# Two feed-forward chunks go up by Strassen's seven products, and the four banks of the ways down become one tile

## The chip, the cores and the metric

The kernel runs on one core of a Trainium2 chip. The metric is the time of one execution on the device in microseconds (us), lower is better. A core has TensorE (PE, matmuls), VectorE (DVE), ScalarE (ACT), GpSimd (POOL) and SyncE (SP, which here only issues DMAs). Each has its own instruction queue, worked off in order, and they wait for each other by semaphores.

## The reference

x is 512 tokens of 1024 features in float32. Two layers; in each a half-step SwiGLU feed-forward, a mixer (an mLSTM in layer 0, a chunked gMLP in layer 1), a second feed-forward and a gated per-layer embedding (PLE), each followed by a layer norm:

```python
for i in range(DEPTH):
    x = layer_norm(DN_ALPHA * x + 0.5 * swiglu_ffn(x, ffn1_wgu[i], ffn1_wd[i]), ...)
    x = layer_norm(DN_ALPHA * x + mix, ...)                  # mlstm_mixer or gmlp_mixer
    x = layer_norm(DN_ALPHA * x + 0.5 * swiglu_ffn(x, ffn2_wgu[i], ffn2_wd[i]), ...)
    x = layer_norm(DN_ALPHA * x + sigmoid(x @ ple_wg[i] + ple_bg[i]) * (p[i] @ ple_wp[i]), ...)

def swiglu_ffn(x, w_gu, w_d):
    g, u = jnp.split(x @ w_gu, 2, axis=-1)
    return (jax.nn.silu(g) * u) @ w_d                        # hidden width 2816
```

## The kernel before, in words

**Products.** A float32 product is made of three matmuls (mm3, lines 277 to 281): high by high, low by high and high by low, where the high part (whi, xh, fhi) is the value rounded to fp32r and the low part (wlo, xl, flo) the rest. The high part is an ACT copy (weights L198, others L284), the low part a DVE subtraction (L207, L285), or, where a stage asks for it, an ACT copy of the negative and an accumulating DMA that POOL issues (L205).

**Weights.** The class Weights streams all weights in one list, W.order: SP loads raw tiles (wraw of 1 MB, three buffers; wquarter of 512 KB for the ways down), fill() splits the next entry as soon as its pool (main, rows, extra and others) has a free pair of tiles, take() hands a pair to PE's code and release() gives it back and calls fill(). The order in which the code calls these sets the order on every queue; there is no scheduler behind it.

**A feed-forward** (ffn, L827) has 22 blocks of 128 hidden columns, in chunks of 2, 4, 4, 4, 4 and 4 blocks. Going up, each block is two tiles (gate and up) of 24 matmuls of 512 columns into a PSUM bank of ps_up (fps); ACT applies silu (sg, L856), DVE multiplies (h, L860). Going down, the h of a whole chunk is a 2 by 2 problem in halves of tokens and output features: class Group (L765) makes it by Strassen's seven products, r = 0 to 6. form() adds quarters of h on DVE (L792 to L797) and splits them (fhi, flo), the weights' quarters are added in place by Weights.forms (L109 to L115), product() runs 12 matmuls (6 in chunk 1, whose chunk before has two blocks) into two PSUM banks (gps), and add() adds a finished product to x (xt), bank by bank (residual, L626 or L628). The seven products of chunk c − 1 stand between the up tiles of chunk c: after the up tile i comes add() of the product before, then silu or multiplication, then product(i) and form(). The last chunk goes down plainly (down, L654): for each of four token tiles 24 matmuls into two banks (dps), then two residuals, a norm and transposes of x back to the form that PE needs (turn_x, L490; DVE steps of the norm to come, affine, L620 and L621, run in the next feed-forward's chunk 1).

**PSUM.** Four banks are for going up (up0 to up3), four are tiles dn0 to dn3, handed out by dn_bank (L295) to groups, to down, to turn_x and to the mixers' and embedding's tiles (vps, gvps L1311, gps of the embedding L1527). Even products of a group write one pair of banks and odd ones the other: product r uses the pair of product r − 2 (and, but for r = 0, 1 and 3, goes on adding to what stands there).

**mLSTM** makes its own way down by a Group for each head, between the tiles of the next head's projections, with the convolution (L1003) on DVE.

## Time and profile before

| what | value |
|---|---|
| median of 3 runs | 2227.38 us (2226.92 to 2227.43) |
| span of the profiled execution | 2225.4 us |
| granted TensorE clock | 9 tenths or more in each of 40 slices |
| DMA | 253.57 MB, mean 114 GB/s |
| a feed-forward chunk of four blocks with a group (219 to 282 us): PE, DVE, ACT busy | 63.00, 40.74, 21.98 us |

The span is that of the profiled execution itself; what the runs' time has beyond it, 2.0 us against their median, lies around it. In the profile a row of a timeline has the start and the duration, the engine, the line of the kernel, the operation and the tiles (written <- read) with their shapes; `x2` joins two instructions that follow each other. The bracket names how long the engine stood idle before and what ended that. A matmul's duration (0.39 us) is longer than the distance to the next one, since matmuls overlap; time on PE is read from the starts.

### The profile page before, as it was taken

The numbers are of one execution on the slowest core, as the hardware profiler recorded it, in microseconds if no ns is written. First come the engines' busy times: TensorE is split into PE (matmuls) and PEld (weight loads), VectorE is DVE, ScalarE is ACT, GpSimd is POOL, SyncE is SP. The second block draws the span as 40 slices with busy tenths as digits, with TensorE's granted clock in tenths as the row PEclk, the third lists the DMA queues.
The fourth block names the chain that finished last, engine by engine and source line by source line (L and its number), as shares of the span: only waits on it lengthen the run. The fifth ranks groups of instructions, "written<-read, shape, count | busy, mean of one in ns | idle before, by whom it ended". The sixth has DMA issues, their size and how long they took to land.

```text
span 2225.4 us, 26475 instructions
## 1 busy us (share of the span) xinstructions
PE 2214.4 (100%) x10517; PEld 1856.1 (83%) x10517; DVE 1557.3 (70%) x2280; ACT 922.2 (41%) x1308; POOL 104.3 (5%) x135
## 2 busy tenths in 40 slices
PE   9999999999999999999999999999999999999998
PEld 8888888888888888888888888888888888888887
DVE  5666667776776786666687766666788778666677
ACT  4333336464646443333345333335345453333332
POOL 1000000111101100000000000000001100000000
PEclk9999999999999999999999999999999999999999
DMA  7422223466847444332233422223437743332221
GB/s 230 130 95 88 95 86 100 100 143 140 160 117 154 130 133 128 98 106 63 99 123 111 134 92 90 95 85 97 140 76 152 164 129 130 117 114 86 85 86 57
DMA packets 206308, 253.57 MB, mean 114 GB/s; under 512 B 5812, under 2 KB 160564, under 8 KB 206184
## 3 DMA queue, kind: packets, MB, share of 16 engines
q1 hardware_dynamic: 168080, 211.83, 29.4%
q0 software_dynamic: 31488, 25.35, 8.4%
q10 hardware_dynamic: 6616, 14.69, 2.0%
q8 instruction: 83, 1.36, 0.2%
q14 instruction: 41, 0.34, 0.0%
HBM read 224.58 MB, written 2.11 MB: 102 GB/s over the span
## 4 chain that ended last, share of the span: by engine, by line
PE 98%; ACT 1%; DMA 0%; DVE 0%; issue 0%; SPq 0%; DVEq 0%
PE fps L279 13%; PE fps L280 13%; PE fps L281 13%; PE gps L279 8%; PE gps L281 8%; PE gps L280 8%; PE dps L279 2%; PE dps L281 2%; PE dps L280 2%; PE gups L279 1%; PE vps L279 1%; PE zps L279 1%; PE zps L281 1%; PE vps L281 1%; PE gvps L279 1%; PE gups L280 1%
## 5 line engine op out<-in xcount | busy, mean ns | idle before, releaser
L279 PE MATMUL fps<-xh,whi 128*128 128x512 f32 x1312 | 510.7, 389 | 0.0
L280 PE MATMUL fps<-xl,whi 128*128 128x512 f32 x1312 | 510.4, 389 | 0.0
L281 PE MATMUL fps<-xh,wlo 128*128 128x512 f32 x1312 | 510.4, 389 | 0.0
L207 DVE TENSOR_TENSOR wlo<-wraw,whi 128x1024 fp32r<-128x1024 f32 (+1 forms) x292 | 352.7, 1218 | 147.9 <-ACT whi L198 146.8
L198 ACT ACTIVATE whi<-wraw 128x1024 fp32r<-128x1024 f32 (+1 forms) x340 | 352.2, 1048 | 179.0 <-PE fps L280 81.6
L207 DVE TENSOR_TENSOR wlo<-wquarter,whi 128x1024 fp32r<-128x1024 f32 (+1 forms) x140 | 156.5, 1118 | 218.2 <-ACT whi L198 218.2
L281 PEld LDWEIGHTS fps<-xh,wlo 128*128 128x128 f32 x1312 | 246.2, 188 | 51.3
L279 PEld LDWEIGHTS fps<-xh,whi 128*128 128x128 f32 x1312 | 246.3, 188 | 51.2
L280 PEld LDWEIGHTS fps<-xl,whi 128*128 128x128 f32 x1312 | 246.3, 188 | 50.6
L198 ACT ACTIVATE whi<-wquarter 128x1024 fp32r<-128x1024 f32 (+1 forms) x140 | 136.3, 974 | 279.8 <-PE gps L281 209.0
L281 PE MATMUL gps<-whi,flo 128*128 128x512 f32 x644 | 251.1, 390 | 0.0
L279 PE MATMUL gps<-whi,fhi 128*128 128x512 f32 x644 | 251.1, 390 | 0.0
L280 PE MATMUL gps<-wlo,fhi 128*128 128x512 f32 x644 | 251.0, 390 | 0.0
L628 DVE TENSOR_TENSOR xt<-xt,gps 128x512 f32<-128x512 f32 x302 | 193.2, 681 | 0.7 <-PE gps L281 0.7
L856 ACT ACTIVATE sg<-fps 128x512 f32<-128x512 f32 x80 | 47.9, 598 | 228.5 <-PE fps L281 224.3
L281 PEld LDWEIGHTS gps<-whi,flo 128*128 128x128 f32 x644 | 120.9, 188 | 25.7
L280 PEld LDWEIGHTS gps<-wlo,fhi 128*128 128x128 f32 x644 | 120.9, 188 | 25.5
L279 PEld LDWEIGHTS gps<-whi,fhi 128*128 128x128 f32 x644 | 120.9, 188 | 25.5
L284 ACT ACTIVATE fhi<-h 128x512 fp32r<-128x512 f32 (+1 forms) x140 | 80.5, 581 | 142.8 <-DVE h L793 54.4
L285 DVE TENSOR_TENSOR flo<-h,fhi 128x512 fp32r<-128x512 f32 (+1 forms) x140 | 87.2, 635 | 42.9 <-ACT fhi L284 42.9
L598 POOL TENSOR_TENSOR rs<-rs,eps_pow 128x1 f32<-128x1 f32 x32 | 20.6, 643 | 1573.6 <-DVE rs L597 1573.6
L501 ACT ACTIVATE xf<-xps,cols 128x128 f32<-128x128 f32 x160 | 59.8, 454 | 53.5 <-PE xps L496 53.5
(306 smaller groups left out, 3625.8 us busy)
## 6 DMA issues: line engine op xcount, KB each, us to landing
wraw<-in_ffn_wgu_dram SPq DMA_DIRECT2D x79, 1024.0 KB, 6.3
wquarter<-in_ffn_wd_dram SPq DMA_DIRECT2D x64, 512.0 KB, 3.7
wraw<-in_ml_w_in_dram SPq DMA_DIRECT2D x24, 1024.0 KB, 5.5
wlo<-wraw POOLq DMA_DIRECT2D x48, 512.0 KB, 6.6
wraw<-in_gm_w_in_dram SPq DMA_DIRECT2D x15, 1024.0 KB, 5.6
wraw<-in_ffn_wgu_dram SPq DMA_DIRECT2D x17, 512.0 KB, 4.0
wraw<-in_ffn_wd_dram SPq DMA_DIRECT2D x8, 1024.0 KB, 4.9
wraw<-in_ml_w_out_dram SPq DMA_DIRECT2D x8, 1024.0 KB, 5.0
```

Of the source, the lines that this page charges most:

```text
L198: self.nc.scalar.activation(hi[:, s], src[:, s], AF.Copy)
L207: self.nc.vector.tensor_sub(lo[:, s], src[:, s], hi[:, s].bitcast(F32))
L279: mm(ps, st[0], mv[0], start=start, stop=False, skip_group_check=more)
L280: mm(ps, st[0], mv[1], start=False, stop=False, skip_group_check=more)
L281: mm(ps, st[1], mv[0], start=False, stop=stop, skip_group_check=more)
L284: sca.activation(hi, src, AF.Copy)
L285: vec.tensor_sub(lo, src, hi.bitcast(F32))
L501: sca.activation(xf[:, k], ps[:, k], AF.Identity, scale=col("ln_g", norm.at + 4 * g + k), bias=col("ln_b", norm.at + 4 * g + k))
L598: pool.tensor_tensor(rs[:, 1:2], rs[:, 0:1], eps_pow, op=OP.pow)
L628: vec.tensor_add(dst, dst, ps)
L856: sca.activation(sg, ps, AF.Silu)
```

## The change

1. Going up in chunks 4 and 5 (UP_FROM): two blocks at a time are a pair, x's features and tokens are halved, and gate and up weights of two blocks form the 2 by 2 problem. Each of seven products is 24 matmuls of 256 columns into half a bank at a time (class UpPair), so 168 of them stand for 96 of 512 columns. The weights' combinations are made in place on the raw loads by DVE (up_forms, four of the seven need additions); the combinations of x by UpForms, in steps of DVE and ACT in chunk 3, two after each up tile from the fourth on (FORM_AT), and last() behind that chunk's last tile. take() collects the sums out of the banks; a group's products stand after every second product going up.
2. Five of the seven lows of each pair (UP_BY_DMA) are made by an ACT copy and an accumulating DMA.
3. The four PSUM tiles dn0 to dn3 become one tile, dn_all, of four banks. dn_bank hands out a slice of it, dn_pair two neighbouring banks, and a group's add() takes both banks of a product in one DVE instruction of 128x2x512.
4. The rows' pool has two buffers for three, a further one (rowsx) is opened late in chunk 5, and the norm's tiles (Norm) are made there too.

```diff
+    def up_forms(self, g, u):
...
+        def s2():
+            vec.tensor_add(quarter(u, 0), quarter(u, 0), quarter(u, 1))
+            vec.tensor_sub(quarter(g, 0), quarter(u, 0), quarter(g, 0))
+            return quarter(g, 0), (g,)
...
+        def s3():
+            vec.tensor_sub(quarter(u, 0), quarter(u, 1), quarter(g, 0))
+            return quarter(u, 0), (u,)
...
+        def s4():
+            vec.tensor_sub(quarter(g, 1), quarter(g, 1), quarter(g, 0))
+            return quarter(g, 1), (g,)
...
+        for _, make in made:
+            self.in_place.add(make)
+        self.by_dma.update(made[r][1] for r in UP_BY_DMA)
+        return [("main", js, make) for js, make in made]
...
-                if low == "dma" and make not in self.in_place:
+                if make in self.by_dma or low == "dma" and make not in self.in_place:
                     self.nc.scalar.activation(lo[:, s], src[:, s], AF.Copy, scale=-1.0)
                     self.nc.gpsimd.dma_start(lo[:, s], src[:, s], accum_op=OP.add)
...
-    def dn_bank(name, pin=False):
+    dn_all = ps_dn.tile([P, 4, 512], F32, name="dn_all", tag="dn_all")
+    def dn_bank(name):
         i = next(i for i in dn_order if i not in pinned.values())
         dn_order.remove(i)
         dn_order.append(i)
...
+    def dn_pair(name):
+        i = next(i for i in dn_order if not {i, i ^ 1} & set(pinned.values())) & 2
+        for j in (i, i + 1):
...
+        pinned[id(pair)] = i
+        pinned[id(pair), 1] = i + 1
+        return pair
...
         del W.order[first:]
         for c, n in enumerate(FFN_CHUNKS):
             down_w = deque(forms(c - 1) if c else ())
+            if c >= UP_FROM:
+                products = []
+                for b in range(starts[c], starts[c] + n, 2):
+                    products += W.up_forms(*(W.add_load(kp(wgu)[:, :, c0:c0 + 2 * P], 2) for c0 in (b * P, HID + b * P)))
+                for s, product in enumerate(products):
+                    W.order.append(product)
+                    if s % 2 == 0:
+                        W.order.append(down_w.popleft())
+                continue
             for i in range(2 * n):
...
-                self.banks.append([dn_bank("gps", True) for _ in range(2)])
-            for e, ps in enumerate(self.banks[r % 2]):
+                self.banks.append(dn_pair("gps"))
+            pair = self.banks[r % 2]
+            for e in range(2):
                 for k in range(self.half):
                     i, j = (e, k) if self.by_tokens else (k, e)
-                    mm3(ps, [a[:, i, j * P:(j + 1) * P] for a in f], [a[:, k] for a in w],
+                    mm3(pair[:, e], [a[:, i, j * P:(j + 1) * P] for a in f], [a[:, k] for a in w],
                         k == 0 and r in (0, 1, 3), k == self.half - 1, r not in (0, 1, 3))
...
             i, j = self.TO[r]
-            for e, ps in enumerate(self.banks[r % 2]):
-                residual(2 * i + e, j, ps, r in self.first)
-                if r >= 5:
-                    unpin(ps)
-    def ffn(layer, k, rows, prepare=None):
-        with stage_pool("forms", 2) as fpool, stage_pool("quarters", Q_BUFS) as qpool, stage_pool("hpool", 2) as hpool:
+            pair = self.banks[r % 2]
+            dst = xt[:, 2 * i:2 * i + 2, j * 512:(j + 1) * 512]
+            if r in self.first:
+                vec.scalar_tensor_tensor(dst, dst, ALPHA, pair, op0=OP.mult, op1=OP.add)
...
+            def x22():
+                for i, s in enumerate(halves):
+                    joined(a[i], 1, 1, s)
+            def t3():
+                for i, s in enumerate(halves):
+                    vec.tensor_sub(b[:, s], a[i], b[:, s])
+            def t1():
+                for i, s in enumerate(halves):
+                    vec.tensor_sub(a[i], a[i], c[:, s])
+            def split_t1():
+                for i, s in enumerate(halves):
+                    split(self.t1[0][:, s], self.t1[1][:, s], a[i])
+            self.steps = [
+                x22, lambda: joined(b, 0, 1), t3, lambda: joined(c, 0, 0), lambda: vec.tensor_add(c, b, c),
+                lambda: sca.activation(f32r(self.t2, late, "whi"), c, AF.Copy), t1, split_t1]
+            def last():
+                split(*self.t3, b)
+                d = [tmp_tile("x_d").rearrange("p (k t) -> p k t", k=2) for _ in range(2)]
+                for i, s in enumerate(halves):
+                    joined(d[i], 1, 0, s)
+                    vec.tensor_sub(d[i], d[i], c[:, s])
+                vec.tensor_sub(f32r(self.t2, late, "wlo"), c, self.t2[0].bitcast(F32))
+                hi, lo = f32r(self.t4, pool, "f1"), f32r(self.t4, pool, "f0")
+                for i, s in enumerate(halves):
+                    split(hi[:, s], lo[:, s], d[i])
+            self.last = last
+            self.right = [self.quarter(0, 0), self.quarter(1, 0), self.t2, self.t1, self.t3,
+                          self.quarter(1, 1), self.t4]
...
+        def product(self, r):
+            w = W.take()
+            c = (0, 1, 0, 3, 0, 3, 0)[r]
+            if r == c:
+                self.at[c], bank = up_bank("ups", True)
+                self.bank[c] = bank.rearrange("p (e c) -> p e c", e=2)
+            ps = self.bank[c]
+            for e in range(2):
+                for k in range(4):
+                    mm3(ps[:, e], [a[:, k, e * P:(e + 1) * P] for a in w], [a[:, k] for a in self.right[r]],
+                        r == c and e == 0 and k == 0, k == 3, r != c or e > 0)
...
+        def take(self, r):
+            bank, part = self.bank, self.part
+            if r in (0, 2, 3):
+                part[r] = tmp_tile("us").rearrange("p (e c) -> p e c", e=2)
+                sca.activation(part[r], bank[3 if r == 3 else 0], AF.Copy)
+            elif r in (1, 5):
+                g = part[r // 5 * 2]
+                vec.tensor_add(g, g, bank[1 if r == 1 else 3])
+                sca.activation(g, g, AF.Silu)
+                if r == 5:
+                    self.gated(1, g, part[3])
+            elif r == 4:
+                vec.tensor_add(part[3], part[3], bank[0])
+            else:
+                self.gated(0, part[0], bank[0])
+            if r in (1, 5, 6):
+                up_held.remove(self.at[{1: 1, 5: 3, 6: 0}[r]])
+        def gated(self, t, g, u):
+            s = slice(256 * t, 256 * t + 256)
+            h = g if self.h is None else self.h[:, :, s]
+            vec.scalar_tensor_tensor(h, g, 0.5, u, op0=OP.mult, op1=OP.mult)
+            if self.h is None:
+                split(*(a[:, :, s] for a in self.parts), h)
...
+            def up_products(c, n, h):
+                nonlocal norm
+                pairs = []
+                for s in range(7 * n // 2):
...
+                    pair.product(r)
+                    group.add()
+                    if r == 5 and h is None:
+                        pair.parts = [W.spare(name).rearrange("p (b t) -> p b t", b=2) for _ in range(2)]
+                        hs.extend([a[:, e] for a in pair.parts] for e in range(2))
+                    pair.take(r)
+                    W.release()
+                    if s % 2 == 0:
+                        group.product()
+                        W.release(kind="rows")
+                        group.form()
+                    if c == LAST and b == n - 2:
+                        if r == 2:
+                            W.open("rowsx", late, 1)
+                        elif r == 4:
+                            norm = Norm(layer, k)
             for c, n in enumerate(FFN_CHUNKS):
                 if c < LAST:
                     h = hpool.tile([P, 4, SEQ], F32, name="h", tag="h")[:, :n]
                 elif prepare is not None:
                     prepare()
-                for i in range(2 * n):
+                if c == UP_FROM - 1:
+                    formed = UpForms(tpool, late)
+                if c >= UP_FROM:
+                    up_products(c, n, h if c < LAST else None)
+                for i in range(2 * n if c < UP_FROM else 0):
                     b = i // 2
                     ps = project()
...
                         group.form()
                     if c == 1 and i < 3:
                         run_affine()
+                    if formed is not None and i >= FORM_AT:
+                        formed.step()
+                        formed.step()
+                if c == UP_FROM - 1:
...
+                        formed.step()
+                    formed.last()
                 if c < LAST:
                     group = Group(h, fpool, c == 0)
                     group.form()
                     group.form()
                 if c == 0:
...
-                if c == 1:
-                    norm = Norm(layer, k)
             return down(hs, False, norm, lazy=layer == 0, defer=prepare is not None)
...
     def ffn_stage(layer, k):
-        with stage_pool("rows", 3) as rows:
-            W.open("rows", rows, 3)
-            ffn(layer, k, rows)
+        with stage_pool("rows", 2) as rows, stage_pool("late") as late:
+            W.open("rows", rows, 2)
+            ffn(layer, k, rows, late)
             W.close("rows")
```

Two places in the order of the built programs. The first is PE at product 1 of the group in layer 0's first feed-forward, chunk 2 (fps: up tile; gps: the banks of the group; whi, wlo, fhi, flo: weights and h forms; in brackets the engines whose count it waits for). Before:

```order
L281 MATMUL fps_938<-xh_87,wlo_773 128x512
L279 MATMUL gps_966<-whi_784,fhi_869 128x512 [waits Activation_49]
L280 MATMUL gps_966<-wlo_785,fhi_869 128x512
L281 MATMUL gps_966<-whi_784,flo_870 128x512 [waits DVE_49]
L279 MATMUL gps_966<-whi_784,fhi_869 128x512
```

After:

```order
L320 MATMUL fps_906<-xh_88,wlo_768 128x512
L318 MATMUL dn_all_86<-whi_807,fhi_846 128x512 [waits DVE_49,Activation_49]
L319 MATMUL dn_all_86<-wlo_808,fhi_846 128x512
L320 MATMUL dn_all_86<-whi_807,flo_847 128x512
L318 MATMUL dn_all_86<-whi_807,fhi_846 128x512
```

The product's first matmul has gained a wait for DVE: its count is that of the add of product 0, which reads the two other banks of dn_all. Before, the DVE wait stands at the third matmul alone, for the form's low. All later up matmuls stand behind it on PE.

The second is DVE at the end of chunk 3 of the same feed-forward, from the last product's add to the low of the next group's first h form (flo_1723 before, flo_1719 now). Before:

```order
L628 TENSOR_TENSOR xt_86<-xt_86,gps_1331 128x512
L628 TENSOR_TENSOR xt_86<-xt_86,gps_1332 128x512
L860 SCALAR_TENSOR_TENSOR h_1303<-sg_1666,fps_1690 128x512
L207 TENSOR_TENSOR wlo_1719<-wraw_1567,whi_1718 128x1024
L285 TENSOR_TENSOR flo_1723<-h_1303,fhi_1722 128x512
L285 TENSOR_TENSOR flo_1727<-h_1303,fhi_1726 128x512
```

After:

```order
L896 TENSOR_TENSOR xt_87<-xt_87,dn_all_86 128x2x512
L1072 SCALAR_TENSOR_TENSOR h_1266<-sg_1640,fps_1671 128x512
L246 TENSOR_TENSOR wlo_1699<-wraw_1490,whi_1698 128x1024
L324 TENSOR_TENSOR xl_89<-x_wlo_1269,xh_88 128x4x256
L915 TENSOR_TENSOR x_d_1704<-xh_88,xl_89 128x512
L946 TENSOR_TENSOR x_d_1704<-x_d_1704,x_f0_1270 128x512
L915 TENSOR_TENSOR x_d_1705<-xh_88,xl_89 128x512
L946 TENSOR_TENSOR x_d_1705<-x_d_1705,x_f0_1270 128x512
L947 TENSOR_TENSOR t_wlo_1710<-x_f0_1270,t_whi_1612 128x1024
L324 TENSOR_TENSOR t_f0_1713<-x_d_1704,t_f1_1712 128x512
L324 TENSOR_TENSOR t_f0_1713<-x_d_1705,t_f1_1712 128x512
L324 TENSOR_TENSOR flo_1719<-h_1266,fhi_1718 128x512
```

Two adds have become one of 128x2x512, and eight instructions of last() (xl, x_d, t_wlo, t_f0) have come between the last up weights' low and the form's low that PE waits for.

More of the change, by code (lines that the diff above doesn't have):

```diff
@@ L45 @@
 PLE_EXTRA = 3
+UP_BY_DMA = (1, 2, 4, 5, 6)
 class Weights:
@@ L363, in ffn_weights @@
         first = len(W.order)
-        for at in range(HB):
-            if at in (0, HB - 1):
+        for at in range(starts[UP_FROM]):
+            if at == 0 or at == starts[UP_FROM] - 1:
                 W.add(*((kp(wgu)[:, :, c0:c0 + P], [slice(None)]) for c0 in (at * P, HID + at * P)))
@@ new lines, in add, with __init__, joined, f32r @@
+            if r >= 5:
+                unpin_pair(pair)
+    class UpForms:
+        def __init__(self, pool, late):
+            f32 = lambda at, tag: at.tile([P, 4, 256], F32, name="x_" + tag, tag=tag)
+            a = [tmp.tile([P, 2, 256], F32, name="x_a", tag="pad", bufs=3) for _ in range(2)]
+            b, c = f32(late, "wlo"), f32(pool, "f0")
+            both = act.tile([P, 2, 4, 256], F32R, name="t1", tag="gb")
+            self.t1, self.t2, self.t4 = [both[:, 0], both[:, 1]], [], []
+            self.t3 = self.quarter(0, 1)
+            whole, halves = slice(0, 4), (slice(0, 2), slice(2, 4))
+            def joined(dst, k, t, s=whole):
+                vec.tensor_add(dst, *(p[:, s].bitcast(F32) for p in self.quarter(k, t)))
+            def f32r(to, at, tag):
+                to.append(at.tile([P, 4, 256], F32R, name="t_" + tag, tag=tag))
+                return to[-1]
+            def x22():
[26 more added lines that the diff above has]
+                          self.quarter(1, 1), self.t4]
+        def quarter(self, k, t):
+            return [a[:, 4 * k:4 * k + 4, 256 * t:256 * t + 256] for a in (xh, xl)]
+        def step(self):
+            if self.steps:
+                self.steps.pop(0)()
@@ L829, in ffn @@
+    def ffn(layer, k, rows, late, prepare=None):
+        with stage_pool("forms", 2) as fpool, stage_pool("quarters", Q_BUFS) as qpool, \
+                stage_pool("hpool", 2) as hpool, stage_pool("tforms") as tpool:
             name = (layer, k)
@@ L1460, in ffn_ple @@
     def ffn_ple(i, last):
-        with stage_pool("rows", 3) as rows:
-            W.open("rows", rows, 3)
+        with stage_pool("rows", 2) as rows, stage_pool("late") as late:
+            W.open("rows", rows, 2)
             ph, pl = [], []
@@ L1550, in ffn_ple @@
                 norm.apply(TB - 1)
-                for kind in ("rows", "rows2", "extra"):
+                for kind in ("rows", "rowsx", "rows2", "extra"):
                     W.close(kind)
```

69 lines of the change are left out of this document (51 added, 18 removed).

## The prediction

> **What bounds the kernel now.** I read the busy times first, then the chain that ended last, then timelines of TensorE (PE) and VectorE (DVE) around the ways down. The page's two rows (engine, busy time, share of the span; and the chain by engine):
> ```profile
> PE 2214.4 (100%) x10517; PEld 1856.1 (83%) x10517; DVE 1557.3 (70%) x2280; ACT 922.2 (41%) x1308; POOL 104.3 (5%) x135
> PE 98%; ACT 1%; DMA 0%; DVE 0%; issue 0%; SPq 0%; DVEq 0%
> ```
> PE is never without work, so matmul time that goes away shortens the run, and any wait that PE gains lengthens it one for one. Everything else was hidden. The question is what the change makes PE wait for.
>
> The timeline of a group of ways down, FFN chunk 3 of layer 0's first FFN: the first matmul of each of the products r = 1 to 5 on PE, the first up matmul behind product 1, and the weight copy that ScalarE (ACT) starts when product 0 ends (start, duration):
> ```profile
> 226.66 0.39 PE L279 MATMUL gps<-whi,fhi 128*128 128x512 f32 x1
> 229.38 0.39 PE L279 MATMUL fps<-xh,whi 128*128 128x512 f32 x1
> 234.82 0.39 PE L279 MATMUL gps<-whi,fhi 128*128 128x512 f32 x1
> 242.98 0.39 PE L279 MATMUL gps<-whi,fhi 128*128 128x512 f32 x1
> 251.14 0.39 PE L279 MATMUL gps<-whi,fhi 128*128 128x512 f32 x1
> 259.30 0.39 PE L279 MATMUL gps<-whi,fhi 128*128 128x512 f32 x1
> ...
> 221.42 1.06 ACT L198 ACTIVATE whi<-wquarter 128x1024 fp32r<-128x1024 f32 x1 [2.12 <-PE gps L281]
> ```
> And DVE's adds of the products r = 0 to 4 to x in the same group:
> ```profile
> 227.57 1.28 DVE L628 TENSOR_TENSOR xt<-xt,gps 128x512 f32<-128x512 f32 x2
> 233.55 1.28 DVE L628 TENSOR_TENSOR xt<-xt,gps 128x512 f32<-128x512 f32 x2
> 243.16 1.28 DVE L628 TENSOR_TENSOR xt<-xt,gps 128x512 f32<-128x512 f32 x2
> 251.32 1.28 DVE L628 TENSOR_TENSOR xt<-xt,gps 128x512 f32<-128x512 f32 x2
> 256.90 1.28 DVE L628 TENSOR_TENSOR xt<-xt,gps 128x512 f32<-128x512 f32 x2
> ```
> A product is 12 matmuls in 229.38 − 226.66 = 2.72 us, 0.2268 us each; products follow every 8.16 us. To be seen: the add of product r−1 ends at 228.85, 234.83, 244.44, 252.60 and 258.18, that is 2.19, 0.01, 1.46 and 1.46 us *after* product r has started, and once 1.12 us before it. Today that costs nothing, since product r writes the other pair of banks and needs only the add of r−2.
>
> **The change: the banks become one tile.** The order of the built programs (in the change's section) shows the decisive point. Before, product r waits for the DVE add that last read its own bank. Now the four banks are one tile, dn_all, and its count is that of the add just before, of product r−1 in the other two banks: of the 287 waits of PE on an earlier reader of this tile, 283 are for a reader of other banks (170 on group adds, 22 on the residuals of the plain ways down, 15 and 17 on the readers of gvps and of the gates in the per-layer embedding, some 30 on turns of x). PE's queue stands in order, so behind each such wait stands all up work. What each costs is how late that reader ends today. Since the chain product end → ACT copy (221.42, released by PE) → DVE low, h forms, add hangs on the product's own end, a delayed product delays the next add by as much: the latenesses add up.
>
> *Chunks 2 and 3.* 2.19 + 0.01 + 1.46 + 1.46 = 5.1 us per group. In chunk 3 DVE also gets the steps of the x forms, two at each tile from the fourth on (about 2.5 us ahead of adds 3 and 4, 1.2 ahead of add 5, by 0.64 to 1.22 us an operation, rows below): 1.46 + 2.5 and −1.12 + 2.5 make it 9.0. Four FFNs: 20 + 36 = **+56**, from 41 (steps hidden) to 72.
>
> *Chunk 1* (halved groups, layer 0's second FFN, products 1 to 4 and the adds before them):
> ```profile
> 804.50 0.39 PE L279 MATMUL gps<-whi,fhi 128*128 128x512 f32 x1
> 811.30 0.39 PE L279 MATMUL gps<-whi,fhi 128*128 128x512 f32 x1
> 818.10 0.39 PE L279 MATMUL gps<-whi,fhi 128*128 128x512 f32 x1
> 824.90 0.39 PE L279 MATMUL gps<-whi,fhi 128*128 128x512 f32 x1
> ```
> ```profile
> 806.23 1.28 DVE L626 SCALAR_TENSOR_TENSOR xt<-xt,gps 128x512 f32<-128x512 f32 x2
> 812.50 1.28 DVE L628 TENSOR_TENSOR xt<-xt,gps 128x512 f32<-128x512 f32 x2
> 819.32 1.28 DVE L626 SCALAR_TENSOR_TENSOR xt<-xt,gps 128x512 f32<-128x512 f32 x2
> 824.15 1.28 DVE L626 SCALAR_TENSOR_TENSOR xt<-xt,gps 128x512 f32<-128x512 f32 x2
> ```
> 3.01 + 2.48 + 2.50 + 0.53 = 8.5 us; three FFNs have the affine steps ahead of these adds, the first has none: **+26**, from 9 (only the first wait stands, DVE then has caught up) to 34 (the first FFN too).
>
> *mLSTM's groups*, three heads (products 1 to 3, then the adds of 0 to 2, the second row being the latter half of its add):
> ```profile
> 474.24 0.39 PE L279 MATMUL gps<-whi,fhi 128*128 128x512 f32 x1
> 482.49 0.39 PE L279 MATMUL gps<-whi,fhi 128*128 128x512 f32 x1
> 490.74 0.39 PE L279 MATMUL gps<-whi,fhi 128*128 128x512 f32 x1
> ```
> ```profile
> 480.73 1.28 DVE L626 SCALAR_TENSOR_TENSOR xt<-xt,gps 128x512 f32<-128x512 f32 x2
> 488.46 0.68 DVE L628 TENSOR_TENSOR xt<-xt,gps 128x512 f32<-128x512 f32 x1
> 492.42 1.28 DVE L626 SCALAR_TENSOR_TENSOR xt<-xt,gps 128x512 f32<-128x512 f32 x2
> ```
> Late by 7.77, 6.65 and 2.96. Here DVE is behind with the convolution, which it works off while PE stands: at least 7.8 per head, at most 17.4; I take 9, near the lower: **+27**.
>
> *Plain ways down, gvps, embedding, turns.* The add of the last product behind product 6, the residual of one token tile, the transposes six matmuls into the next, and the groups of the other two readers:
> ```profile
> 337.51 1.28 DVE L628 TENSOR_TENSOR xt<-xt,gps 128x512 f32<-128x512 f32 x2
> ...
> 349.91 0.67 DVE L628 TENSOR_TENSOR xt<-xt,dps 128x512 f32<-128x512 f32 x1
> ```
> ```profile
> 330.02 0.39 PE L279 MATMUL gps<-whi,fhi 128*128 128x512 f32 x1
> ...
> 350.43 0.60 PE L496 MATMUL xps<-ident,xt 128*128 128x128 f32 x4
> ```
> ```profile
> L1531 DVE TENSOR_TENSOR pg<-gps,bgb 128x512 f32<-128x512 f32 (+1 forms) x18 | 11.2, 623 | 4.8 <-PE gps L281 4.7
> L1314 DVE TENSOR_TENSOR gvf<-gvps,gvb 128x512 f32<-128x512 f32 x16 | 11.0, 687 | 6.7 <-PE gvps L281 6.6
> ```
> The tile started at 350.43 − 6 × 0.2268 = 349.07, the residual before it ended at 350.58: 1.5 us late; I take 1.7 for each of three a way down. Its first tile waits for the last add, which ends 338.79 − 332.74 = 6.05 us after product 6; only one 2.88 us up product lies between, so 3.2. Four FFNs 4 × (3.2 + 5.2) = 34, the two mixers 6 each (estimate): **+46**, from 25 to 60. A gvps or gate tile now waits for the add behind the previous one, 0.69 or 0.62 long and begun after its end: 0.9 each, 32 of them, **+29** (20 to 45). Turns: **+8** (0 to 15).
>
> **The change: chunks 4 and 5 by seven products.** 256-column matmuls stand in before's last stages; the first and the seventeenth of a run:
> ```profile
> 365.59 0.28 PE L279 MATMUL sup<-xh,whi 128*128 128x256 f32 x1
> ...
> 367.51 0.28 PE L280 MATMUL sup<-xl,whi 128*128 128x256 f32 x1
> ```
> 1.92 / 16 = 0.120 us. A pair of blocks takes 7 × 24 × 0.120 = 20.16 instead of 96 × 0.2268 = 21.77: −1.61, 16 pairs, **−26**. The Trainium skill (TensorE: Matmul & The Clock Gate, Back-to-back issue gap) lists 262 cycles for 256 columns and 518 for 512; an estimate from its figures gives 2.4 per pair, and the sum would be 12 us lower. The trace's 0.120 against 0.2268 decides.
>
> Start of chunk 4: the last x forms (last()) stand on DVE ahead of the first h form's low, which PE needs at the third matmul of the group. Durations:
> ```profile
> L207 DVE TENSOR_TENSOR wlo<-wraw,whi 128x1024 fp32r<-128x1024 f32 (+1 forms) x292 | 352.7, 1218 | 147.9 <-ACT whi L198 146.8
> L285 DVE TENSOR_TENSOR flo<-h,fhi 128x512 fp32r<-128x512 f32 (+1 forms) x140 | 87.2, 635 | 42.9 <-ACT fhi L284 42.9
> ```
> Three operations of 1024 (1.22) and eight of 512 (0.64 to 0.68) are 9.0 us after the last up tile; PE has 24 × 0.120 + 2 × 0.2268 = 3.3 to do. Stall 5.7, **+23** in four FFNs (0 if ACT or DVE ran ahead, to 30).
>
> The adds in these chunks: products come every 5.76 + 2.72 = 8.48 us, but DVE has more ahead of each add: per pair four forms and two lows of 1.22 and five sums of 0.68 (10.7 us) for four lows and two products with silu before (6.2), and ACT 12 weight copies of 1.06 for 4. Some forms overwrite a load that a low by DMA still reads, and DVE stands for it. Nearest rows are chunk 2's 5.1 and chunk 3's 9.0; I take 10 for each of eight groups, **+80** (5.1 to 14: 41 to 112).
> ```profile
> wlo<-wraw POOLq DMA_DIRECT2D x48, 512.0 KB, 6.6
> ...
> 219.00:282.00 63.00, 63.00 (x280) 52.16 (x279) 40.74 (x49) 21.98 (x27) 0.00 (x0) 1.00 0.26 84
> ```
> The lows by DMA land after 6.6 us, and the DMA engines are 26% busy in such a chunk; 80 more of 512 KB I cost at nothing beyond this. Two-bank adds, one for two: about 1.22 for 1.28, nothing. The third buffer that the rows' pool loses, and the norm that is built later, I cost at nothing: a row's copy already starts only when a product has ended (221.42). POOL, 5% busy, gets 80 issues, with nothing queued behind them before the way down's norm.
>
> **The sum.** 56 + 26 + 27 + 46 + 29 + 8 − 26 + 23 + 80 = +269 us on the profiled 2225.4 (span; the runs' median of 2227.38 has 2 us around it): 2227 + 269 = **2496 us**. All low ends together give +133 (2360), all high ends +394 (2621).
>
> **Rivals.**
> (a) *The adds get ahead*: the waits are there, but bite nowhere, because DVE loses the lows that go by DMA and one of two adds. Then 2227 − 26 = 2201, with the start of chunk 4 2224: faster. It needs the add to end within the 5.44 us of up work behind its product; today it ends 7.47 us after it (221.38 to 228.85). The lows leave DVE in chunks 4 and 5 alone, so 5.1 us per group stay in the others. The Trainium skill (PSUM — Partial Sum Buffer, PSUM bank collisions raise a hardware error) says accesses to different banks run clean and asks for guards by bank; by that rule product r need not wait, and this time would come out. The order agrees that the wait is not one of banks, but it stands in the program. Chance 0.06.
> (b) *DVE catches up*: stalls give it time, only the first wait of each group stays: 2.2 in chunks 2 to 5 (16 groups, 35), 9 in chunk 1, 23 in mLSTM, 25 + 20 from the rest, less 26, plus 23: +109, **2336**. Against: ACT's copies hang on the product's end, so waiting gives no lead. Chance 0.12.
> (c) *DMA binds in chunks 4 and 5*: with five lows and two loads of 1 MB per 29.7 us, a low lands twice as late as 6.6, and DVE's form and the adds behind it stand up to 6.6 more, once a pair: 16 × 6.6 = 106, **2600**. The Trainium skill (DMA: Bandwidth & Descriptors, Issuing engines are not separate DMA queues) has all issuers share the same 16 engines, which speaks for it; 26% busy speaks against. Chance 0.12.
> Forecast 0.70.
>
> **How the numbers follow.** The point is the forecast's 2496. All ends at once are unlikely, so its own range is about half as wide (2430 to 2560); with (b) and (c) at 0.12 each the range has to reach towards both, and leaves out (a) and the far half of each: 2360 to 2600. A measurement tells about 0.2% (4.5 us) from no change. Faster takes most of (a): 0.05; same the rest, 0.02; slower 0.93.
>
> **What would show it.** PE's idle time before gps products goes from nothing to over 100 us, released by DVE's two-bank add; the chain that ended last shows DVE at over 10%; PE busy falls by some 26 us; the product period of chunk 2 is 10.3, 8.2, 9.6, 9.6 instead of 8.16. I am wrong if PE's waits are on ACT's weight copies or DMA instead, if chunk 2 keeps its 8.16, or if the time is below 2300.

## The result, and the profile after

The changed kernel takes 2747.22 us (median of 4 runs, 2745.69 to 2748.92) against 2227.27 us before (2226.92 to 2227.43): a ratio of 1.2336, 95% interval 1.2318 to 1.2353, 520 us slower. The forecast was 2496 us, the range 2360 to 2600: the direction and the waits behind it were right, and about half of the added time was missing, most of it a cost of the waits that the sum had no term for.

Rows of the changed kernel's page: busy times, the granted TensorE clock in 40 slices, the matmuls of the groups, their adds, and the lows by DMA (in the last row KB each and us to landing).

```profile
PE 2364.1 (86%) x11669; PEld 1973.0 (72%) x11669; DVE 1675.2 (61%) x2261; ACT 1090.2 (40%) x1508; POOL 171.8 (6%) x215
PEclk9998999999999999999999998999999999999999
L318 PE MATMUL dn_all<-whi,fhi 128*128 128x512 f32 x660 | 294.8, 447 | 204.1 <-DVE xt L896 136.7
L896 DVE TENSOR_TENSOR xt<-xt,dn_all 128x1024 f32<-128x1024 f32 x151 | 183.2, 1213 | 3.3 <-PE dn_all L320 3.3
wlo<-wraw POOLq DMA_DIRECT2D x128, 512.0 KB, 5.3
```

PE is idle for 14% of the span, and it is *busy* for 150 us more than before (2364.1 for 2214.4), though its work is 26 us shorter. The groups' matmuls last 447 ns on average where they lasted 390. PE waits, above all ahead of the first matmul on dn_all, and its matmuls have become slower. Both show in one group, chunk 2 of layer 0's first feed-forward (PE, products 0 and 1; start, duration, in the bracket the idle time and what ended it):

```profile
103.78 0.39 PE L318 MATMUL dn_all<-whi,fhi 128*128 128x512 f32 x1
...
114.26 0.71 PE L318 MATMUL dn_all<-whi,fhi 128*128 128x512 f32 x1 [2.16 <-DVE xt L896]
114.77 0.63 PE L319 MATMUL dn_all<-wlo,fhi 128*128 128x512 f32 x1
115.19 0.63 PE L320 MATMUL dn_all<-whi,flo 128*128 128x512 f32 x1
...
117.75 0.40 PE L320 MATMUL dn_all<-whi,flo 128*128 128x512 f32 x1
117.99 0.39 PE L318 MATMUL dn_all<-whi,fhi 128*128 128x512 f32 x1
```

and the add that product 1 waits for, on DVE:

```profile
112.90 1.21 DVE L896 TENSOR_TENSOR xt<-xt,dn_all 128x1024 f32<-128x1024 f32 x1
```

The add ends at 114.11 and product 1 starts at 114.26. The predicted wait was 2.19 us, the measured one is 2.16. What was not predicted stands in the next rows: the matmuls behind the wait follow each other every 0.42 to 0.43 us (114.77, 115.19) instead of 0.2268, for some 3.4 us, and then 0.23 to 0.24 again. Windows of the changed kernel over this place (busy time of PE, PEld, DVE, ACT and POOL, then the granted clock, the DMA share and GB/s):

```profile
100.00:110.00 10.00, 10.00 (x46) 8.29 (x45) 5.20 (x5) 2.61 (x3) 0.00 (x0) 1.00 0.00 0
110.00:120.00 10.00, 7.84 (x28) 6.01 (x27) 6.30 (x9) 1.75 (x3) 0.00 (x0) 0.83 0.00 0
```

The clock falls in the window with the wait. In the trace's record of the clock it is only ever 1.0 or 0.5; it is at 0.5 for 320.7 us of this run, in 68 stretches, against one stretch of 6.8 us in the kernel before, which begins at 2220.6 us as its work runs out. The page's slices are too coarse for it: all but two still read 9.

What PE waited for in the changed kernel, its longest entries (us in total, times, longest us):

```profile
PE dn_all L318 <- DVE xt L896: 160.4, 76, 6.7
PE dn_all L318 <- DVE xt L697: 46.9, 22, 3.9
PE dn_all L318 <- DVE pad L1216: 22.9, 3, 7.6
PE dn_all L318 <- DVE xt L894: 22.1, 9, 4.8
PE dn_all L318 <- ACT fhi L323: 20.7, 4, 5.4
PE dn_all L318 <- DVE pg L1749: 13.5, 14, 2.4
PE dn_all L320 <- DVE flo L324: 9.1, 8, 1.5
```

Group adds (L896, and L894 where the add also scales x), the residuals of the plain ways down (L697), mLSTM's groups (the first wait of each of three heads, put down here to the convolution's pad, a step behind the add), the h forms (L323, L324) and gates (L1749): the list that the prediction worked through.

An account from all matmul rows of a trace: a wait is every place where PE stood for over 0.05 us, counted from start to start less 0.2268 us (behind a matmul of 512 columns that is 0.16 us more than its bracket, which counts from the matmul's end); the clock's part is half of the time at 0.5 in which PE ran. All in us, for the profiled execution:

| kernel | work on PE against before | waits | clock | sum with 2225.4 | span |
|---|---|---|---|---|---|
| before | 0 | 1.4 | 0 | 2227 | 2225.4 |
| changed | −26 | 397.5 | 130.8 | 2728 | 2747.2 |
| one tile and two-bank adds alone (e12) | 0 | 292.5 | 75.2 | 2593 | 2608.7 |
| all but these (e4) | −26 | 97.8 | 27.0 | 2324 | 2330.2 |
| two pairs of banks alone (e10) | 0 | 69.8 | 19.1 | 2314 | 2316.1 |

The sums come within 0.7% of the spans. Of the 19 us that are missing in the changed kernel some 17 lie right behind the waits: from the first matmul behind a wait to the second it is 0.32 us at full clock (mean of 115 waits) instead of 0.2268, and 0.575 at half (32 waits) instead of 0.427.

### The profile page after: what moved, and what is told of

Same layout as the page of the kernel before. It is cut to its first block, busy times and chain, and to the rows that moved or that the text cites. A ratio compares the mean times of both kernels' runs of the same rounds, so it can differ in the third digit from the quotient of the medians.

```text
span 2747.2 us, 29349 instructions
## 1 busy us (share of the span) xinstructions
PE 2364.1 (86%) x11669; PEld 1973.0 (72%) x11669; DVE 1675.2 (61%) x2261; ACT 1090.2 (40%) x1508; POOL 171.8 (6%) x215
## 5 line engine op out<-in xcount | busy, mean ns | idle before, releaser
L318 PE MATMUL dn_all<-whi,fhi 128*128 128x512 f32 x660 | 294.8, 447 | 204.1 <-DVE xt L896 136.7
L318 PE MATMUL fps<-xh,whi 128*128 128x512 f32 x800 | 315.2, 394 | 0.0
L319 PE MATMUL fps<-xl,whi 128*128 128x512 f32 x800 | 314.1, 393 | 0.0
L320 PE MATMUL fps<-xh,wlo 128*128 128x512 f32 x800 | 312.8, 391 | 0.0
L320 PE MATMUL dn_all<-whi,flo 128*128 128x512 f32 x660 | 284.8, 431 | 9.1 <-DVE flo L324 9.1
L319 PE MATMUL dn_all<-wlo,fhi 128*128 128x512 f32 x660 | 283.7, 430 | 0.0
L896 DVE TENSOR_TENSOR xt<-xt,dn_all 128x1024 f32<-128x1024 f32 x151 | 183.2, 1213 | 3.3 <-PE dn_all L320 3.3
L319 PEld LDWEIGHTS dn_all<-wlo,fhi 128*128 128x128 f32 x660 | 139.9, 212 | 27.2
L323 ACT ACTIVATE fhi<-h 128x512 fp32r<-128x512 f32 (+1 forms) x140 | 81.0, 582 | 187.2 <-DVE h L862 53.0
L318 PE MATMUL ups<-xh,whi 128*128 128x256 f32 x512 | 146.0, 285 | 2.3 <-DVE us L1004 2.3
L319 PE MATMUL ups<-xl,whi 128*128 128x256 f32 x512 | 145.6, 284 | 0.0
```

The source lines that it names most:

```text
L318: mm(ps, st[0], mv[0], start=start, stop=False, skip_group_check=more)
L319: mm(ps, st[0], mv[1], start=False, stop=False, skip_group_check=more)
L320: mm(ps, st[1], mv[0], start=False, stop=stop, skip_group_check=more)
L323: sca.activation(hi, src, AF.Copy)
L896: vec.tensor_add(dst, dst, pair)
```

## The experiments

Theory A: PE waits for readers of other banks, since the four banks are one tile, and the granted clock falls behind such waits. Theory B: the work going up by seven products (forms, copies, DMAs) is what costs.

**e1_onetile**, the kernel before with one tile:

```diff
+    dn_all = ps_dn.tile([P, 4, 512], F32, name="dn_all", tag="dn_all")
...
-        bank = ps_dn.tile([P, 512], F32, name=name, tag=f"dn{i}")
+        bank = dn_all[:, i]
```

> The kernel before with the four banks of the ways down as slices of one tile, and nothing else of the change. Theory A (waits on other banks' readers, and the granted clock that falls to a half after them): about 310 us of waits (16 groups in chunks 2 to 5 of 6.2, chunk 1 26, mLSTM 27, ways down and turns about 105, gvps and gates 54) and a third of that again by the clock: 2640 us, from 2560 to 2700. Theory B (the seven products going up, their forms on DVE and their copies and DMAs are what costs): one tile alone costs under 100 us, below 2330.

2613.77 us, ratio 1.1739 (1.1723 to 1.1755), in theory A's range. Two lines of code and no other work cost 387 us: B is out as the main cause. From the list of its waits (us, times, longest):

```profile
PE dn_all L279 <- DVE xt L629: 142.8, 84, 3.9
PE dn_all L279 <- DVE xt L627: 22.4, 9, 4.9
```

These are the adds and residuals, which in the kernel before nobody waited for.

**e12_onetile_run**, e1 with a product added from both banks in one instruction, so the whole of the change on the side of the ways down:

```diff
-            for e, ps in enumerate(self.banks[r % 2]):
-                residual(2 * i + e, j, ps, r in self.first)
...
+            pair = self.banks[r % 2]
+            dst = xt[:, 2 * i:2 * i + 2, j * 512:(j + 1) * 512]
...
+                vec.tensor_add(dst, dst, pair)
```

> As e1_onetile, with a product added from two banks in one instruction (the whole of the change on the side of the ways down). One add of 1.14 for two of 1.28: each wait for an add 0.14 shorter at some 80 of them, 2600 us (2590 to 2614). It also settles whether the whole change is the sum of its sides: 2747 less this one against e4_four's 110.

2607.07 us, ratio 1.1709 (1.1693 to 1.1725), in the expected range: 380 us over before, 7 less than e1. The two-bank add by itself is a small gain.

**e4_four**, the changed kernel with four tiles and two adds again:

```diff
-    dn_all = ps_dn.tile([P, 4, 512], F32, name="dn_all", tag="dn_all")
+    dn_four = [ps_dn.tile([P, 512], F32, name="dn", tag=f"dn{k}") for k in range(4)]
...
-        pair = dn_all[:, i:i + 2]
+        pair = dn_four[i:i + 2]
...
+            for e, ps in enumerate(pair):
+                residual(2 * i + e, j, ps, r in self.first)
```

> The changed kernel with four tiles of one bank and two adds a product as before; all else of the change is in. Theory A: 2227 - 26 + 22 for the start of chunk 4 and 10 for clock and late forms: 2233 us (2215 to 2260). Theory B: over 2450, since the work going up is all there.

2337.14 us, ratio 1.0493 (1.0479 to 1.0508): 110 us over before, where about 6 were expected, between the ranges of both theories. So A holds for 380 of the 520 us, the rest of the change costs 110 instead of nothing, and 30 appear only when both are there. The account shows where most of these 30 are: the waits add up (292.5 + 97.8 = 390 for 397.5), the clock's part does not (75.2 + 27.0 = 102 for 130.8). What PE waited for in e4:

```profile
PE dn L318 <- ACT fhi L323: 35.9, 8, 5.5
PE dn L318 <- ACT wquarter L323: 18.8, 4, 5.8
PE dn L320 <- DVE flo L324: 11.6, 8, 2.4
PE ups L320 <- DMA wlo<-wraw: 9.6, 7, 2.2
PE ups L318 <- ACT us L984: 9.3, 14, 1.5
```

The first h form of the groups in chunks 4 *and* 5 (8 times, fhi and flo), the split of the last h ahead of the plain way down (4 times), and the products going up.

**e3_pairs**, the changed kernel with two tiles of two banks:

```diff
+    dn_two = [ps_dn.tile([P, 2, 512], F32, name="dn", tag=f"dn{k}") for k in range(2)]
...
-        return dn_all[:, i]
+        return dn_two[i // 2][:, i % 2]
...
-        pair = dn_all[:, i:i + 2]
+        pair = dn_two[i // 2][:, 0:2]
```

> The changed kernel with two tiles of two banks for the one of four; adds still take two banks in one instruction. Theory A: groups no longer wait for the other pair; what is left is the gain of 26, the stall at the start of chunk 4 of 5.4 four times, waits inside a pair at gvps and gates, some clock: 2265 us (2235 to 2300). Theory B: it keeps most of its 520 us, over 2450.

2420.91 us, ratio 1.0872 (1.0857 to 1.0887), far over theory A's 2265 (2300 at most) and under theory B's 2450: the group adds are gone from the waits, but tiles handed out one bank at a time still wait for their neighbour, and e4's 110 us were not known yet.

**e10_before_pairs**, the kernel before with the pairs and the two-bank adds:

> The kernel before with two tiles of two banks, and a product added from two banks in one instruction; nothing of the work going up. e3_pairs less e4_four is 84 us, so theory A expects 2227 + 75 = 2300 us (2280 to 2320): waits inside a pair at gvps, gates and turns. If these cost only together with the work going up: under 2245.

2319.41 us, ratio 1.0416 (1.0402 to 1.0430), at the upper end of the range. Its longest waits:

```profile
PE dn L506 <- DVE xl L515: 13.4, 6, 3.8
PE dn L279 <- DVE xl L515: 10.6, 4, 3.9
PE dn L279 <- DVE pg L1546: 8.8, 7, 2.4
PE dn L279 <- DVE gvf L1329: 6.4, 6, 1.6
```

Turns of x, gates and gvps: the users of single banks. Two tiles of two banks, with the two-bank adds, cost 93 us by themselves.

**e2_fill**, e1 with matmuls that nobody reads ahead of the products that wait:

```diff
+FILL = (0, 10, 1, 7, 7, 0, 0)
...
+            if self.half == 2 and self.fill and r:
+                fill = up_bank("fill")
+                for k in range(FILL[r]):
+                    nc.tensor.matmul(fill, xh[:, k % 8, 0:P], xh[:, k % 8], start=True, stop=True)
```

> As e1_onetile, but ahead of the products 1, 2, 3 and 4 of each feed-forward group of twelve matmuls PE runs 10, 1, 7 and 7 matmuls of 512 columns on xh into a free bank of the way up, which nobody reads: 25 x 0.2268 = 5.7 us more matmul work a group, about as long as its waits of 5 to 6. Theory A, with the clock as the second cost: the work fits into the waits, the clock stays full there, and the run is FASTER than e1_onetile by the clock's share of these 16 groups, 16 x 2.9 = 46 us (20 to 70). If the slow matmuls behind a wait have another cause than idle PE (the banks, the data), it is as slow as e1_onetile or up to 20 us slower.

2606.65 us (2605.38 to 2607.99) against e1's 2613.77 (2612.57 to 2617.64): 91 us more matmul work, and 7 us *less* time. The adds' waits went from 142.8 us to:

```profile
PE dn_all L280 <- DVE xt L630: 61.0, 36, 3.7
```

By the account the waits fell by 89.5 and the clock's part by 10.2 (71.5 to 61.3). The direction is A's, the size a sixth of what was expected: in e1 only 8 of the 16 waits of 2.2 us ahead of product 1 are followed by the lower clock, and none of the 35 of some 1.4 us, so these groups had little to win. The last section shows what decides it.

**e9_fill4**, e4 with 24 such matmuls ahead of product 0 in chunks 4 and 5:

```diff
+                    if s == 0:
+                        fill = up_bank("fill")
+                        for m in range(24):
+                            mm(fill, xh[:, m % 8, 0:P], xh[:, m % 8], start=True, stop=True)
```

> As e4_four, with 24 matmuls of 512 columns on xh (5.44 us, read by nobody, into a free bank of the way up) ahead of product 0 of the groups in chunks 4 and 5, where PE waits 5.5 + 0.7 or 3.4 + 2.1 us eight times and runs slow behind. If idle PE is what halves the granted clock: the work fits into the waits and the 17 us of slow matmuls behind them go, 2320 us (2312 to 2330), with 44 us more work on PE. If the clock falls for another reason: 2337 or up to 8 us more.

2346.90 us, ratio 1.0541 (1.0527 to 1.0556): 10 us slower than e4, outside of both ranges. Most of the waits ahead of product 0 went (4.9 us of e4's 47.5 are left), but others grew: the fill itself waits, and the products going up behind it:

```profile
PE ups L318 <- DVE us L1001: 15.5, 4, 3.9
PE fill L1042 <- DVE h L1001: 13.5, 4, 5.1
PE ups L318 <- DVE h L1001: 11.3, 4, 2.8
```

Waits fell by 25 for 44 us of fill, and the clock's part stayed (27.0, 26.1), since it now fell behind the new waits. As a test of the clock's cause by the time, this run decides nothing.

**e5_early**, e4 with the first h form of chunks 4 and 5 made behind product 5 of the group before:

```diff
+                        if s == 10 and c < LAST:
+                            early = Group(h, fpool, False)
+                            early.form()
...
```

> As e4_four, but the first h form of the group in chunks 4 and 5 is made three products earlier (behind product 5 of the group before), since it needs the first two blocks alone. Theory A2 (e4_four's rest of 110 us is first of all the first product of a group that waits for its form, which stands on ACT and DVE behind last() in chunk 4 and behind weight forms and loads in chunk 5: in its profile 8 waits of 5.5 and 0.7 or 3.4 and 2.1, 47 us, with some 15 of clock): 2337 - 62 = 2275 us (2260 to 2295). Rival (the copies and lows of the weights are late by as much, so PE waits there instead): 2325 or more.

2342.29 us, ratio 1.0522 (1.0508 to 1.0537), no gain: the rival won. The group no longer waits, and PE stands one product later instead, for ACT's copy of a bank of the products going up:

```profile
PE ups L318 <- ACT us L984: 58.3, 26, 7.0
```

**e6_swap**, e5 with the two halves of the tokens exchanged in the seven products (`t = 1 - t` in UpForms.quarter and in gated):

> As e5_early, and the two halves of the tokens change places in the seven products, so that the last product finishes the half that the plain way down needs last. In e4_four PE waits there 5.8 us four times for the split of the last h: theory A2 expects 19 us and some 8 of clock less than e5_early, about 2248 (2235 to 2270). If the way down waits for its weights or for the adds anyway: no change against e5_early.

2326.61 us, ratio 1.0446 (1.0432 to 1.0461), 16 us faster than e5: the way down's 14.9 us wait for the last h is gone from its list. With e5 without effect, the absolute expectation (2248) fails. The rows of the two engines show why the wait only moved. PE, DVE and ACT of e6 at the start of chunk 4:

```profile
239.15 0.58 PE L318 MATMUL ups<-xh,whi 128*128 128x256 f32 x1 [5.58 <-ACT us L985]
```

```profile
233.50 1.28 DVE L697 TENSOR_TENSOR xt<-xt,dn 128x512 f32<-128x512 f32 x2
234.70 0.68 DVE L988 TENSOR_TENSOR us<-us,ups 128x512 f32<-128x512 f32 x1
235.29 1.22 DVE L151 TENSOR_TENSOR wraw<-wraw 128x1024 f32<-128x1024 f32 x1
```

```profile
232.23 0.63 ACT L323 ACTIVATE fhi<-h 128x512 fp32r<-128x512 f32 x1 [2.68 <-DVE h L862]
235.41 0.63 ACT L989 ACTIVATE us<-us 128x512 f32<-128x512 f32 x1 [2.55 <-DVE us L988]
236.61 1.06 ACT L237 ACTIVATE whi<-wraw 128x1024 fp32r<-128x1024 f32 x1 [0.56 <-DVE wraw L151]
237.57 1.04 ACT L243 ACTIVATE wlo<-wraw 128x1024 fp32r<-128x1024 f32 x1
238.52 0.58 ACT L985 ACTIVATE us<-ups 128x512 f32<-128x512 f32 x1
```

ACT stands for DVE's h form, then for DVE's sum, then for DVE's weight form, and only then comes the copy (238.52) that frees the bank for PE. Over this chunk (213 to 280 us) neither engine is full, DVE with 50.3 and ACT with 39.3 of 67 us; each stands in order behind the other, and one product going up gives them 2.88 us of cover where an up tile gave 5.44. This is read from the rows; no run takes it out as a whole.

**e11_forms**, e6 with four additions of last() moved into the steps:

> As e6_swap, with four of last()'s additions (2.7 us on DVE) moved into the steps between chunk 3's tiles, which begin a tile earlier. If last() is what the first products of chunk 4 wait for: 2.7 us less four times and a little clock, 2313 us (2305 to 2320). If the weights' forms and copies decide alone: 2326 as e6_swap.

2320.93 us (2318.63 to 2324.07), ratio 1.0427 (1.0412 to 1.0441): 6 us faster than e6, about half of what was expected and just outside of the range; last() is one part of the late start of chunk 4.

**e7_dvelow**, e6 with all lows on DVE (`UP_BY_DMA = ()`):

> As e6_swap with all seven lows of a pair made by DVE, none by DMA. If lows by DMA hold up the raw buffers, and with them loads and forms (PE waits 9.6 us for them in e4_four): up to 20 us faster than e6_swap. If DVE is the tighter one (it gets 5 x 1.22 us a pair of 29.7 us, 98 us of work in all): 10 to 50 us slower. I lean to slower by 15.

2348.43 us, ratio 1.0546 (1.0531 to 1.0560), 22 us slower than e6, the side that was leaned to. PE no longer waits for any low by DMA, but more for DVE and ACT:

```profile
PE ups L318 <- ACT us L985: 61.6, 12, 8.4
PE ups L318 <- DVE us L1003: 21.6, 4, 5.7
PE ups L318 <- ACT whi L237: 16.4, 4, 4.3
```

The lows by DMA are worth their place. DMA is not what binds.

**e8_up5**, e6 with the last chunk alone by seven products (`UP_FROM = 5`):

> As e6_swap with only the last chunk by seven products (the forms of x move to chunk 4): half of the gain of 26 and half of the waits at products going up: if those waits outweigh the gain, it is faster than e6_swap, about 2235 (2220 to 2255); if the gain outweighs them, slower by up to 13.

2296.30 us, ratio 1.0308 (1.0294 to 1.0322): 30 us faster than e6, so the waits outweigh the gain, but 61 us over the expected 2235. The waits were not halved (61.8 us by the account, for 92.8 in e6): the 2.3 and 5.6 us that PE stands at the start of chunk 4 in e6 come again at the start of chunk 5 here. One chunk going up this way costs 69 us over before and the second a further 30, although each saves 13 us of matmuls. No version here beats the kernel before.

The rows' pool and the later norm (part 4 of the change) are in every version with work going up, and no run takes them out, so their share of the 69 us is open. In e8 PE stands 12 us in the plain ways down and turns for norms and residuals, where it did not stand in the kernel before.

## Why the prediction was right and wrong

**Right: which wait, and that it is paid.** The step from the built order (283 waits on readers of other banks) to the time held: e1 changes only that and costs 387 us. Lateness read from the trace of before gave the size of most of the groups' waits well. For chunk 2 it said 2.19, 0.01, 1.46, 1.46 and none; PE then waited 2.16, none, 1.44, 1.43 and 1.12 by the brackets (product 1 above, and these, products 3 to 5 of the changed kernel):

```profile
134.10 0.47 PE L318 MATMUL dn_all<-whi,fhi 128*128 128x512 f32 x1 [1.44 <-DVE xt L896]
143.98 0.47 PE L318 MATMUL dn_all<-whi,fhi 128*128 128x512 f32 x1 [1.43 <-DVE xt L896]
153.54 0.47 PE L318 MATMUL dn_all<-whi,fhi 128*128 128x512 f32 x1 [1.12 <-DVE xt L896]
```

mLSTM's heads waited 7.6 each and then hardly again: its lower end, 7.8, was right, the 9 that was taken a little high, and the remark that DVE catches up while PE stands held.

**Wrong: the sum has no term for the clock.** "Any wait that PE gains lengthens it one for one" is the step that failed: the sum took matmuls at 0.2268 us throughout, and every wait as costing its own length. Behind a wait the granted clock can fall to a half; that is 131 us in the changed kernel, the largest part of the missing 251. It is also why PE's busy time rose by 150 us, where a fall by some 26 was named as a sign. The trace of before could hardly show it: PE was never idle there, and the clock falls only at its very end. But the prediction put hundreds of waits into that stream and did not ask what they do to the clock. The Trainium skill (TensorE: Matmul & The Clock Gate, Part 1: The HAM clock gate) describes just this, a clock at a half after an idle window of about 3.4 us; the prediction quoted that page for another figure. The trace agrees on the two values, on the window of 3.41 us and on the spacing (0.427 us for 512 columns at half), but the window need not be idle throughout, see the last section.

**The terms of the sum against the account.** All in us; the last two rows had no term at all.

| term | forecast | changed kernel |
|---|---|---|
| group adds in chunks 2 and 3 | 56 | 72.5 |
| group adds in chunk 1 | 26 | 24.3 |
| mLSTM's groups | 27 | 24.4 |
| group adds in chunks 4 and 5 | 80 | 62.3 |
| h forms at the start of chunk 4 (in chunk 5) | 23 (0) | 25.5 (6.8) |
| products going up, gMLP's groups | 0 | 2.5, 10.6 |
| plain ways down, turns | 46 + 8 | 107 |
| gvps, gates and vps | 29 | 54 |
| other waits | 0 | 8 |
| half clock | none | 131 |
| first matmul behind a wait | none | some 17 |

The groups with forms and products going up have 229 us for 212, but that they agree within a tenth is in part luck: chunks 2 and 3 came out 16 higher and the adds of chunks 4 and 5 18 lower. All waits together are 397.5 us for 295 in the sum.

**Wrong: the plain ways down, turns, gates and gvps.** They had 83 us in the sum and have 161 in the account. In e12, without the work going up, these are 89 and 54, so the price by place was too low and not only disturbed by the rest: turns were given 8 without a row, and a gvps or gate wait 0.9 us where the 38 of them average 1.4, some of them on the steps of a turn of x that reads another bank (xl, L574) and not on the add itself.

**Wrong: the wait ahead of product 5 in chunks 2 and 3.** Product 5 was to wait not at all in chunk 2 and 1.4 us in chunk 3; it waited 1.1 and 3.3. DVE's rows ahead of the add of product 4, chunk 2, first before, then changed, show that the latenesses do not only add up, since the order on DVE shifts too:

```profile
130.03 1.23 DVE L207 TENSOR_TENSOR wlo<-wquarter,whi 128x1024 fp32r<-128x1024 f32 x1 [1.01 <-ACT whi L198]
131.18 0.68 DVE L285 TENSOR_TENSOR flo<-h,fhi 128x512 fp32r<-128x512 f32 x1
...
148.17 1.23 DVE L246 TENSOR_TENSOR wlo<-wquarter,whi 128x1024 fp32r<-128x1024 f32 x1 [4.34 <-ACT whi L237]
149.31 2.35 DVE L246 TENSOR_TENSOR wlo<-wraw,whi 128x1024 fp32r<-128x1024 f32 x2
151.58 0.69 DVE L324 TENSOR_TENSOR flo<-h,fhi 128x512 fp32r<-128x512 f32 x1
```

Two lows of up weights now stand between the quarter's low and the form's, and the add comes 2.3 us later behind its product. Why they come to stand there was not followed up.

**Wrong in both directions: chunks 4 and 5.** The adds took less than they were priced at. The stall at the start was sized rightly (25.5 for 23), but chunk 5 has one too. In e4, without the waits on other banks, forms, the last h ahead of the way down and products going up cost 98 us where the sum had 23. The term "DVE has more ahead of each add" looked at DVE's load; what e6's rows show is that ACT and DVE wait for each other in turn.

**The rivals.** (a), adds that get ahead, is out. (b), a DVE that catches up, is right for mLSTM alone. (c), DMA, is out: lows by DMA landed after 5.3 us, not 13, and e7 without them is slower. Of the signs that were named, DVE's share of the chain that ended last came out at 5%, not over 10%.

## What to carry to other kernels

Before joining buffers into one tile, count which waits the joined tile adds, read from the trace how late each of their readers is, and add up: that gave most single waits of the groups here, and missed those for which the order on the feeding engine shifts. Then charge the waits that leave the matmul engine idle for more than about 1.8 us in one stretch of 3.41 us for the slower matmuls behind them as well. Work that is taken off the bounding engine counts only if the engines that feed it, standing in order behind each other, still fit into the shorter time between its pieces.

## What the runs showed of the hardware

The granted clock falls after much shorter waits than expected, and where a wait lies in time decides whether it falls. In each of the 14 traces all stretches at 0.5 begin on one grid of 3.413 us (to within 2.2 ns) that runs through the whole execution. Take the windows of this grid at full clock, from 20 us after the start to the last matmul, and the time for which PE stands in each by the brackets: behind the 9019 windows with less than 1.80 us the clock never fell; behind 55 with 1.80 to 1.95 us it fell 23 times; behind all 284 with more it fell. At 0.5 the next window is at full clock again if PE stands for less than 0.6 us in this one (306 of 308), and stays at 0.5 if it stands for more than 0.8 us (101 of 101).

The wait of chunk 2 that is shown above (112.10 to 114.26) lies whole in the window from 110.92 to 114.33, and the clock is at 0.5 from 114.33 to 117.74. In e1 the wait ahead of product 1 is 2.17 us long sixteen times. Eight times it has over 1.9 us in one window, and the clock falls behind each; eight times a border of the grid leaves at most 1.85 us on either side, and it falls behind none. The instructions and the banks are the same each time, so neither makes the difference. A window at 0.5 in which PE works throughout costs 1.7 us.

Two sides of a change that each leave waits cost more together than apart, by 30 us here, and nearly all of it is clock: 131 us for 75 and 27. Which windows the two sides fill together was not worked out.
